# One decoder layer on one core: the attention and conv output projections in 512-column products, halves summed on the way out

## The chip, the core and the metric

The kernel runs on one core of a Trainium2 chip. The core has a matrix engine (PE, with its weight loads shown as PEld), a vector engine (DVE), a scalar engine (ACT), GpSimd (POOL) and a queue engine (SP) that issues the loads. PE reads operands from SBUF and writes results to PSUM, of which the kernel uses eight banks, each 512 float32 values wide on 128 partitions. DVE and ACT read PSUM and work through their instructions strictly in the order of the program; so does PE. The engines wait for each other by semaphores.

The metric is the device time of one execution in microseconds (us), as the median of several runs.

## What is computed

One layer of a hybrid decoder on 256 tokens of width 1024, in float32:

```python
proj  = x @ w_in[l]                   # q, k, v, B, C, h and two gates
y_att = moba_attention(q, k, v) @ w_attn_out[l]
y_cnv = (gate_b * causal_dwconv(gate_c * h_in, conv_w_mix[l])) @ w_conv_out[l]
mix   = (g_att * y_att + g_cnv * y_cnv) @ w_o[l]
x     = layer_norm(DEEPNORM_ALPHA * x + mix, ln1_g[l], ln1_b[l])
u     = causal_dwconv(x @ w_up[l], conv_w_ffn[l])
f     = (jax.nn.silu(u[..., :D_FF]) * u[..., D_FF:]) @ w_down[l]
x     = layer_norm(DEEPNORM_ALPHA * x + f, ln2_g[l], ln2_b[l])
```

The attention has 8 heads of 64, and with 256 tokens a single causal block. The change concerns `y_att`, `y_cnv` and the gated sum of the two.

## The kernel before

**Products in three parts.** Every float32 operand is split into a high part (ACT copies it into the type `fp32r`) and a low part (DVE subtracts the high part from the original). A product is then high x high + high x low + low x high, added up in PSUM. For an operand b of 256 tokens there are two forms. The plain one issues three products of 256 columns for each block of 128 rows of the contraction. The other (`cols_wide`, line 333, and `cols_narrow`, line 340) needs b's high and low parts side by side: one product of 512 columns multiplies the weight's high part with both, so that the bank's columns 0 to 255 take high x high and 256 to 511 take high x low; a second product of 256 columns adds low x high to the first half. Whoever empties the bank must add the two halves: ACT copies the second half out, DVE adds the first to it. The input projections for conv and gates and the feed-forward's up projection use this form before the change; the output projections of attention and conv use the plain one.

**Weights.** All weights come in a fixed order of units of 128 x 1024 values, two to a load of 1 MB into one of three raw buffers (line 175, on SP's queue). Splitting a unit takes an ACT copy (`split_h`, line 192, or line 219 by way of `hl_split`) and a DVE subtraction (`split_l`, line 197, or line 220). Nine buffers each hold the high and the low parts. A raw buffer is loaded anew when both units in it are split. In the order of units stand: the gates' 16 units; four pairs `ao`, `co`, `ao`, `co` (attention's and conv's output weights, each unit 512 rows by 256 columns), eight units of W_o, the first four up units, the rest of the feed-forward.

**The order by hand.** The program is written in slots, one for each unit; a slot issues its PE products, then weight copies on ACT and weight low parts on DVE for units some four or five ahead, then what is registered for it by `at` (ACT's part ahead of the weight copies, DVE's behind the low parts). In the gates' slots this is the sum of a gate's halves (lines 648 and 652) and the sigmoid (line 655).

**The stage of the change.** Lines 701 to 714: eight banks y0 to y7, each 128 output columns of both branches for all 256 tokens. `unit_cols` fills columns 256 to 511 of a bank with conv's part (12 products of 256 columns) and then columns 0 to 255 with attention's (12 more). Ahead of a bank the loop issues the splits due (`ahead`) and, for the bank two before, the split of its result (`mix_hl`). Behind it `mix` multiplies the bank by both gates on DVE straight from PSUM (line 694) and adds the two halves (line 695). The result is split into `mT`. The inputs are `aT` (attention, lines 460 to 468) and `yT` (conv, lines 624 to 628), each laid out as part, block, token.

Then come the W_o products for tokens 0 to 127 (eight units, two banks, six products a unit), in whose loop the splits for the coming units and the last two `mix_hl` are issued; the residual and the first layer norm of these rows on DVE (lines 742 to 726) beside the W_o products of tokens 128 to 255; the transposes of the normalized x1 (line 786) and the first up products.

**PSUM.** Four banks (`acc`) hold accumulations that stay long, four (`ps`) serve everything short: scores, transposes, the y banks. Ahead of the feed-forward the four are given back and opened anew as two pairs of banks (`ps_pair`).

Of the kernel before, what the change touches and what calls it, by code (L numbers as in the profile page):

```python
# [137 lines left out]
def layer_kernel(ctx: ExitStack, tc: tile.TileContext, x, wpack, cpack, ln1_g, ln1_b, ln2_g, ln2_b, out):  # L138
    nc = tc.nc

    cst = ctx.enter_context(tc.tile_pool(name="cst", bufs=1))
    big = ctx.enter_context(tc.tile_pool(name="big", bufs=1))
# [3 lines left out]
    single = ExitStack()  # L146
# [61 lines left out]
    def split(u, eng=None):  # L208
        if u < len(units) and units[u]["h"] is None:
            split_start(u)  # L210
            split_part(u, 0, units[u]["shape"][0], eng)
        elif u < len(units) and units[u]["l"] is None:
            split_l(u)

    def low(l, src, h):
        nc.vector.tensor_tensor(l, src, h.bitcast(F32), op=ALU.subtract)

    def hl_split(h, l, src, eng=None):
        nc.scalar.activation(h, src, AF.Copy)  # L219
        (eng or nc.vector).tensor_tensor(l, src, h.bitcast(F32), op=ALU.subtract)  # L220
# [94 lines left out]
                mm3(banks[t], ah[:, k0 + k, t * P:(t + 1) * P], al[:, k0 + k, t * P:(t + 1) * P],  # L315
                    un["h"][:, k, :], un["l"][:, k, :], first and k == 0, last and k == nk - 1)

    def unit_cols(u, o, bh, bl, n0=0):

        un = units[u]  # L320
        nk = un["shape"][0]
        for k in range(nk):
            wh, wl = un["h"][:, k, n0:n0 + P], un["l"][:, k, n0:n0 + P]
            nc.tensor.matmul(o, wh, bh[:, k, :], start=k == 0, stop=False)  # L324
            nc.tensor.matmul(o, wh, bl[:, k, :], start=False, stop=False)  # L325
            nc.tensor.matmul(o, wl, bh[:, k, :], start=False, stop=k == nk - 1)  # L326

    def cols_wide(u, bank, b):


        un = units[u]
        for k in range(un["h"].shape[1]):
            nc.tensor.matmul(bank, un["h"][:, k, :], b[:, k].rearrange("p a s -> p (a s)"), start=k == 0, stop=False)  # L333

    def cols_narrow(u, bank, b):

        un = units[u]
        nk = un["l"].shape[1]
        for k in range(nk):
            nc.tensor.matmul(bank[:, 0:S], un["l"][:, k, :], b[:, k, 0], start=False, stop=k == nk - 1)  # L340

    def cols_pair(u, second, banks, b):

# [3 lines left out]
            cols_narrow(u, banks[1], b)  # L347

    LA = 4
    cur = {"u": 0}  # L350

    def ahead(u):
        for v in range(cur["u"], u + LA + 1):
            split(v)
        cur["u"] = max(cur["u"], u + LA + 1)


    qk = big.tile([P, 2, 2, AW], F32, tag="rows", name="qk")
# [1 line left out]
    vpt = big.tile([P, 3584], F32R, tag="c16", name="vpt")  # L360
    vp = vpt[:, 0:2048].rearrange("p (a t n) -> p a t n", a=2, t=2)
    PT = vpt[:, 2048:3584].rearrange("p (a j n) -> p a j n", a=2, j=2)
    aT = big.tile([P, 2, 4, S], F32R, tag="d8", name="aT")
    yT = big.tile([P, 2, 4, S], F32R, tag="e8", name="yT")

    def rope(t):
        xv = qk[:, t].rearrange("p a (h d) -> p (a h) d", d=HD)[:, :, 0:16].rearrange("p h (i f) -> p h i f", i=2)
# [27 lines left out]
    SB, SM, PR = {}, {}, {}  # L395
# [64 lines left out]
    def attend_h(p):  # L460
        for j in range(2):
            hs = slice(j * HD, (j + 1) * HD)
            nc.scalar.activation(aT[hs, 0, p, :], PR[p, "o"][hs, j * 256:(j + 1) * 256], AF.Copy)

    def attend_l(p):
        for j in range(2):
            hs = slice(j * HD, (j + 1) * HD)
            low(aT[hs, 1, p, :], PR[p, "o"][hs, j * 256:(j + 1) * 256], aT[hs, 0, p, :])

# [4 lines left out]
    def at(u, part, f, *a):  # L474
        beside.setdefault(u, {}).setdefault(part, []).append((f, a))

    done = {"h": 0, "l": 0}

    def slot(u, products=None):


        if products:
            products()
        mine = beside.pop(u, {})
        for f, a in mine.get("pe", []) + mine.get("act", []):
            f(*a)
        while done["h"] <= u + LA + 1:
            if units[done["h"]]["h"] is None:
                split_h(done["h"])
            done["h"] += 1  # L490
        while done["l"] <= u + LA:
            if units[done["l"]]["l"] is None:
                split_l(done["l"])
            done["l"] += 1
        for f, a in mine.get("dve", []):
            f(*a)
# [18 lines left out]
    for p in range(4):  # L515
        s = C0 + 4 + 3 * p
# [3 lines left out]
        s = C0 + 7 + 5 * p  # L520
# [28 lines left out]
    banks = [[acc_bank(f"{m}{t}") for t in range(2)] for m in "qk"] + [[ps_bank(f"v{t}") for t in range(2)]]  # L549
# [40 lines left out]
    CB = {}  # L590
# [31 lines left out]
        nc.vector.tensor_tensor(t, CB["s", "b", pr], t, op=ALU.mult)  # L622

    def conv4_act(pr):
        nc.scalar.activation(yT[:, 0, 2 * pr:2 * pr + 2, :], CB["t", pr], AF.Copy)

    def conv4_dve(pr):
        low(yT[:, 1, 2 * pr:2 * pr + 2, :], CB["t", pr], yT[:, 0, 2 * pr:2 * pr + 2, :])

    for pr, (c1, c2, c3, c4) in enumerate(((6, 10, 11, 13), (13, 16, 18, 21))):  # L630
        at(C0 + c1, "dve", conv1, pr)
# [12 lines left out]
    gates = None  # L644
# [12 lines left out]
    for j in range(16):  # L657
        u = U[("g", 0)] + j
# [15 lines left out]
    for j in range(0, 16, 2):  # L674
        if j == 2:
            gates = big.tile([P, 8, 2, S], F32, tag="b16", name="gates")
        GB[j], GB[j + 1] = two_units(U[("g", 0)] + j, [f"g{j + e}" for e in range(2)])

    for e in range(2):
        slot(U[("g", 0)] + 16 + e)  # L680
    cur["u"] = done["l"]


    ln1 = big.tile([P, 2, D], F32, tag="d8", name="ln1")
    for i, g in enumerate((ln1_g, ln1_b)):
# [1 line left out]

    mT = big.tile([P, 2, KT, S], F32R, tag="c16", name="mT")

    M = {}  # L690

    def mix(i, bank):
        t = scratch([P, 2, S], f"m{i}")
        nc.vector.tensor_tensor(t, gates[:, i], bank.rearrange("p (a t) -> p a t", a=2), op=ALU.mult)
        nc.vector.tensor_tensor(t[:, 0], t[:, 0], t[:, 1], op=ALU.add)
        M[i] = t[:, 0]

    def mix_hl(i):
        hl_split(mT[:, 0, i, :], mT[:, 1, i, :], M.pop(i))

    for half in range(2):
        for e in range(2):
            ua, uc = U[("ao", half)] + e, U[("co", half)] + e
            for n in range(2):
                i = half * 4 + e * 2 + n
                if i > 1:
                    mix_hl(i - 2)
                ahead(uc + n - 1)
                bank = ps_bank(f"y{i}")
                unit_cols(uc, bank[:, 256:512], yT[:, 0], yT[:, 1], n * P)  # L710
                unit_cols(ua, bank[:, 0:256], aT[:, 0], aT[:, 1], n * P)
                if i == 0:
                    slot(uc + n)
                mix(i, bank)


    def norm_stats(r, stats, pieces):
# [43 lines left out]
    st1 = [tmp.tile([P, 4, 6], F32, tag="stats", name=f"stats{t}", bufs=2) for t in range(2)]  # L761
    banks = [acc_bank(f"o0{nh}") for nh in range(2)]
    for k in range(8):
        for v in range(cur["u"], min(U["wo"] + k + LA + 1, U["up0"] + 1)):
            split(v)
            cur["u"] = v + 1
        wo_rows(k, 0, banks)
        if k < 2:
            mix_hl(6 + k)
    for nh in range(2):  # L770
        residual(0, nh, banks[nh], xr, r1[0], st1[0], nh, nh * 512, nh * 512 + 512)
    norm1(0, r1[0], st1[0])
# [6 lines left out]
    for k in range(4, 8):  # L779
        wo_rows(k, 1, banks, (0,))  # L780

    def x1_transpose(t, cs=(0, 1)):
        for c in cs:
            b = ps_bank(f"x1t{t}{c}")
            for j in range(4):
                nc.tensor.transpose(b[:, j * P:(j + 1) * P], x1[:, t, (4 * c + j) * P:(4 * c + j + 1) * P], ident)
            hl_split(x1T[:, 4 * c:4 * c + 4, 0, t * P:(t + 1) * P], x1T[:, 4 * c:4 * c + 4, 1, t * P:(t + 1) * P],
                     b.rearrange("p (j t) -> p j t", j=4))
# [60 lines left out]
        wo_rows(k, 1, banks, (1,))  # L849
    residual(1, 1, banks[1], xr, r1[1], st1[1], 1, 512, 1024)  # L850
    norm1(1, r1[1], st1[1])
    cur["u"] = U["up0"] + 4
    u0 = U["up0"]
    rows = {}

    def up0_rows(t):
        bank = acc_bank("up0_1") if t else ps_bank("up0_0")
        for c in range(4):
            if t == 0 and c == 3:
                x1_transpose(1, (0,))  # L860
            unit_rows(u0 + c, 2 * c, {t: bank}, x1T[:, :, 0], x1T[:, :, 1], c == 0, c == 3, ts=(t,))
        rr = scratch([P, 512], f"up0r_{t}")
        rows[t] = rr
        return bank, rr
# [3 lines left out]
    nc.scalar.activation(r0, b0, AF.Copy)  # L868
    for v in range(4, 8):
        split(u0 + v)  # L870
    cur["u"] = u0 + 8
    b1, r1 = up0_rows(1)
    nc.scalar.activation(r1, b1, AF.Copy)
    for i in range(2):
        PB[i] = acc_bank(f"pb{i}")
    single.close()
    pairs = ctx.enter_context(tc.tile_pool(name="pairs", bufs=2, space=bass.MemoryType.PSUM))

    def ps_pair(name):
        return pairs.tile([P, 2, 512], F32, tag="pair", name=name)  # L880

    def up0_T(i):
        for a in range(2):
# [33 lines left out]
    seq = []  # L917
    for c in range(1, NP // 2):
        for e in range(2):
            i = 2 * c + e  # L920
# [4 lines left out]
                seq.append(("d", d, U[("dn", d // 2)] + d % 2))  # L925
    for d in range(NP - TAIL, NP):
        seq.append(("t", d, U[("dn", d // 2)] + d % 2))
    done = {"h": cur["u"] - seq[0][2], "l": cur["u"] - seq[0][2]}
    def slot(k, stages):


# [114 lines left out]
```

## Time and profile before

| | us |
|---|---|
| median of 3 runs (lowest, highest) | 368.86 (368.48, 370.68) |
| the profiled execution | 369.0 |
| its span in the trace | 367.1 |
| PE busy | 358.0 |
| DVE busy | 294.9 |
| ACT busy | 217.0 |

The time of an execution is a little longer than the span that the trace covers. The profile's lines name the kernel's line (L333), the engine, the operation, and output and inputs by the program's names without their numbers, so that `y` stands for all of y0 to y7. In a timeline the first number is the start in us from the span's start and the second the length of the entry, which may hold several instructions (x2, x3); square brackets give idle time of the engine ahead of it and what ended that.

### The profile page before, as it was taken

Reading aid. Unit: us, or ns where it says so; the run is one execution under the profiler, and the core shown is the slowest. Engines: PE = TensorE matmul, PEld = TensorE weight load, DVE = VectorE, ACT = ScalarE, POOL = GpSimd, SP = SyncE. Lnnn points to the kernel's source line nnn. Section 1 sums busy time; section 2 is a strip of 40 time slices with the busy share of each in tenths; the row PEclk is TensorE's granted clock in tenths of the full one; section 3 lists DMA queues with packets and bytes.
Section 4 is the critical chain, followed back from the end, with each engine's and each line's share of the span. In section 5 each row is a group of like instructions: output and inputs, shape, how many; then the busy total and the mean of one; then the engine's idle time right before and its main releaser. Section 6 shows DMA issues by size and latency. Waiting matters only on the chain.

```text
span 367.1 us, 5335 instructions
## 1 busy us (share of the span) xinstructions
PE 358.0 (98%) x2022; PEld 312.2 (85%) x2022; DVE 294.9 (80%) x510; ACT 217.0 (59%) x372; POOL 7.0 (2%) x26
## 2 busy tenths in 40 slices
PE   8999999999999999999999999999999999999991
PEld 7888888888888899988888888888888888888891
DVE  4696887788895679869769988987869696999784
ACT  4685776747867654634266666575657566676300
POOL 2000000000000000102000000000000000000000
PEclk9999999999999999999999999999999999999998
DMA  7978565333853634596360835448182645662011
GB/s 263 356 292 318 180 225 211 114 114 129 331 214 130 221 124 137 190 357 224 124 223 12 341 121 221 153 193 309 46 334 90 254 140 204 228 237 108 0 59 57
DMA packets 11241, 69.63 MB, mean 190 GB/s; under 512 B 1232, under 2 KB 1616, under 8 KB 4176
## 3 DMA queue, kind: packets, MB, share of 16 engines
q1 hardware_dynamic: 10496, 67.00, 50.0%
q0 software_dynamic: 576, 2.10, 1.8%
q8 instruction: 16, 0.26, 0.3%
q10 hardware_dynamic: 144, 0.20, 0.1%
q14 instruction: 9, 0.07, 0.1%
HBM read 68.24 MB, written 1.05 MB: 189 GB/s over the span
## 4 chain that ended last, share of the span: by engine, by line
PE 97%; DVE 1%; DMA 1%; DVEq 0%; SPq 0%; issue 0%
PE pb L333 20%; PE pb L340 10%; PE g L333 8%; PE d L305 5%; PE d L306 5%; PE d L307 5%; PE g L340 4%; PE q L555 3%; PE k L555 3%; PE v L555 3%; PE b L333 2%; PE y L326 2%; PE y L325 2%; PE y L324 2%; PE c L333 2%; PE o L307 2%
## 5 line engine op out<-in xcount | busy, mean ns | idle before, releaser
L197 DVE TENSOR_TENSOR wl<-raw,wh 128x1024 fp32r<-128x1024 f32 x90 | 109.8, 1221 | 23.3 <-ACT wh L192 22.7
L192 ACT ACTIVATE wh<-raw 128x1024 fp32r<-128x1024 f32 x90 | 94.5, 1055 | 22.7 <-DMA raw<-in_wpack 22.6
L333 PE MATMUL pb<-x1T,wh 128*128 128x512 f32 x320 | 76.2, 390 | 0.0
L333 PEld LDWEIGHTS pb<-x1T,wh 128*128 128x128 f32 x320 | 59.7, 188 | 12.1
L220 DVE TENSOR_TENSOR wl<-raw,wh 128x1024 fp32r<-128x1024 f32 (+1 forms) x38 | 38.0, 1037 | 7.4 <-ACT wh L219 7.1
L340 PEld LDWEIGHTS pb<-x1T,wl 128*128 128x128 f32 x320 | 41.0, 191 | 1.6
L340 PE MATMUL pb<-x1T,wl 128*128 128x256 f32 x320 | 41.5, 283 | 0.0
L219 ACT ACTIVATE wh<-raw 128x1024 fp32r<-128x1024 f32 (+1 forms) x38 | 32.9, 904 | 14.3 <-DMA raw<-in_wpack 8.5
L333 PE MATMUL g<-xT,wh 128*128 128x512 f32 x128 | 31.4, 393 | 0.0
L305 PE MATMUL d<-wh,f 128*128 128x512 f32 x80 | 31.3, 391 | 0.0
L306 PE MATMUL d<-wl,f 128*128 128x512 f32 x80 | 31.3, 391 | 0.0
L307 PE MATMUL d<-wh,f 128*128 128x512 f32 x80 | 31.1, 389 | 0.0
L333 PEld LDWEIGHTS g<-xT,wh 128*128 128x128 f32 x128 | 23.3, 188 | 4.5
L807 ACT ACTIVATE fb<-pb 128x512 f32<-128x512 f32 x20 | 11.9, 595 | 23.8 <-PE pb L340 23.8
L825 DVE SCALAR_TENSOR_TENSOR fc<-fb,consts,fc 128x254 f32<-128x254 f32 x40 | 19.3, 484 | 1.4
L823 DVE SCALAR_TENSOR_TENSOR fc<-fb,consts,fc 128x255 f32<-128x255 f32 x40 | 19.1, 478 | 0.0
L817 ACT ACTIVATE fc<-fb,consts 128x256 f32<-128x256 f32 x40 | 17.9, 496 | 0.4 <-DVE fb L811 0.4
L307 PEld LDWEIGHTS d<-wh,f 128*128 128x128 f32 x80 | 15.0, 188 | 3.2
L305 PEld LDWEIGHTS d<-wh,f 128*128 128x128 f32 x80 | 15.1, 189 | 2.7
L306 PEld LDWEIGHTS d<-wl,f 128*128 128x128 f32 x80 | 15.1, 189 | 2.6
L340 PEld LDWEIGHTS g<-xT,wl 128*128 128x128 f32 x128 | 16.4, 191 | 0.6
L340 PE MATMUL g<-xT,wl 128*128 128x256 f32 x128 | 16.6, 283 | 0.0
(183 smaller groups left out, 606.1 us busy)
## 6 DMA issues: line engine op xcount, KB each, us to landing
raw<-in_wpack SPq DMA_DIRECT2D x55, 1024.0 KB, 4.9
raw<-in_wpack SPq DMA_DIRECT2D x6, 896.0 KB, 5.5
xr<-in_x SPq DMA_DIRECT2D x1, 1024.0 KB, 7.6
ln<-in_ln_g POOLq DMA_DIRECT2D x2, 512.0 KB, 5.6
ln<-in_ln_b POOLq DMA_DIRECT2D x2, 512.0 KB, 6.2
raw<-in_wpack SPq DMA_DIRECT2D x3, 256.0 KB, 3.4
raw<-in_wpack SPq DMA_DIRECT2D x1, 512.0 KB, 5.8
out<-x SPq DMA_DIRECT2D x2, 256.0 KB, 2.1
```

What stands on the lines that cost most here:

```text
L192: nc.scalar.activation(units[u]["h"], raw_of(u), AF.Copy)
L197: nc.vector.tensor_tensor(units[u]["l"], raw_of(u), units[u]["h"].bitcast(F32), op=ALU.subtract)
L219: nc.scalar.activation(h, src, AF.Copy)
L220: (eng or nc.vector).tensor_tensor(l, src, h.bitcast(F32), op=ALU.subtract)
L305: nc.tensor.matmul(o, ah, bh, start=start, stop=False)
L306: nc.tensor.matmul(o, ah, bl, start=False, stop=False)
L307: nc.tensor.matmul(o, al, bh, start=False, stop=stop)
L333: nc.tensor.matmul(bank, un["h"][:, k, :], b[:, k].rearrange("p a s -> p (a s)"), start=k == 0, stop=False)
L340: nc.tensor.matmul(bank[:, 0:S], un["l"][:, k, :], b[:, k, 0], start=False, stop=k == nk - 1)
L555: nc.tensor.matmul(banks[m][t], (xl if p == 2 else xh)[:, k, t * P:(t + 1) * P], wl if p == 1 else wh, start=k == 0 and p == 0, stop=k == ...
L823: nc.vector.scalar_tensor_tensor(c[:, 1:S], pb[:, a * S:a * S + S - 1], w_ffn(1, j), c[:, 1:S], op0=ALU.mult, op1=ALU.add)
L825: nc.vector.scalar_tensor_tensor(c[:, 2:S], pb[:, a * S:a * S + S - 2], w_ffn(0, j), c[:, 2:S], op0=ALU.mult, op1=ALU.add)
```

## The change

The y banks go over to the wide and narrow form. Each y now takes a pair of banks, conv's in the second and attention's in the first, in 8 products of 512 columns and 8 of 256. ACT copies the second halves of both banks into a scratch tile (`mix_act`), DVE adds the first halves (`mix_sum`), multiplies by the gates and adds the branches (`mix_dve`); ACT and DVE split the result (`mix_h`, `mix_l`). `aT` and `yT` are laid out as block, part, token, so that the two parts lie side by side.

The stage is written as slots like those ahead of it: bank i's copy, sum and gating belong to the slot of bank i+1, its split to that of bank i+2. A new list `first` puts the sum ahead of the weight low parts of its slot. The two slots without products that stood ahead of the first bank go. The W_o loop for tokens 0 to 127 becomes slots too; splitting stops at the first up unit as before (`SPLIT_LAST`). The four short banks are given back and opened as two pairs ahead of the y stage instead of ahead of the feed-forward, and the transposes of x1 and the first up bank use halves of such pairs.

```diff
-    def cols_wide(u, bank, b):
+    def cols_wide(u, bank, b, n0=0):
...
-            nc.tensor.matmul(bank, un["h"][:, k, :], b[:, k].rearrange("p a s -> p (a s)"), start=k == 0, stop=False)
+            nc.tensor.matmul(bank, un["h"][:, k, n0:n0 + P], b[:, k].rearrange("p a s -> p (a s)"), start=k == 0, stop=False)
...
-            nc.tensor.matmul(bank[:, 0:S], un["l"][:, k, :], b[:, k, 0], start=False, stop=k == nk - 1)
+            nc.tensor.matmul(bank[:, 0:S], un["l"][:, k, n0:n0 + P], b[:, k, 0], start=False, stop=k == nk - 1)
...
-    aT = big.tile([P, 2, 4, S], F32R, tag="d8", name="aT")
-    yT = big.tile([P, 2, 4, S], F32R, tag="e8", name="yT")
+    aT = big.tile([P, 4, 2, S], F32R, tag="d8", name="aT")
+    yT = big.tile([P, 4, 2, S], F32R, tag="e8", name="yT")
...
+    SPLIT_LAST = U["up0"]
...
-        while done["h"] <= u + LA + 1:
+        while done["h"] <= min(u + LA + 1, SPLIT_LAST):
...
-        while done["l"] <= u + LA:
+        for f, a in mine.get("first", []):
+            f(*a)
+        while done["l"] <= min(u + LA, SPLIT_LAST):
...
-    for e in range(2):
-        slot(U[("g", 0)] + 16 + e)
-    cur["u"] = done["l"]
...
+    single.close()
+    pairs = ctx.enter_context(tc.tile_pool(name="pairs", bufs=2, space=bass.MemoryType.PSUM))
...
-    def mix(i, bank):
-        t = scratch([P, 2, S], f"m{i}")
-        nc.vector.tensor_tensor(t, gates[:, i], bank.rearrange("p (a t) -> p a t", a=2), op=ALU.mult)
+    def mix_act(i):
+
+        t = M["t", i] = scratch([P, 2, S], f"m{i}")
+        nc.scalar.activation(t, M[i][:, :, S:2 * S], AF.Copy)
+
+    def mix_sum(i):
+        t = M["t", i]
+        nc.vector.tensor_tensor(t, M.pop(i)[:, :, 0:S], t, op=ALU.add)
+
+    def mix_dve(i):
+        t = M["t", i]
+        nc.vector.tensor_tensor(t, gates[:, i], t, op=ALU.mult)
         nc.vector.tensor_tensor(t[:, 0], t[:, 0], t[:, 1], op=ALU.add)
...
+    def mix_h(i):
+        nc.scalar.activation(mT[:, 0, i, :], M["t", i][:, 0], AF.Copy)
+
+    def mix_l(i):
+        low(mT[:, 1, i, :], M.pop(("t", i))[:, 0], mT[:, 0, i, :])
...
+    def mixed(i):
+
+        M[i] = ps_pair(f"y{i}")
+        half, e, n0 = i // 4, i // 2 % 2, i % 2 * P
+        parts = [(U[("co", half)] + e, M[i][:, 1], yT, n0), (U[("ao", half)] + e, M[i][:, 0], aT, n0)]
+        if i == 0:
+            for part in parts:
+                cols_wide(*part)
+                cols_narrow(*part)
+        else:
+            for f in (cols_wide, cols_narrow):
+                for part in parts:
+                    f(*part)
+
+    for i in range(8):
+        at(Y0 + i + 1, "act", mix_act, i)
+        at(Y0 + i + 1, "first", mix_sum, i)
+        at(Y0 + i + 1, "dve", mix_dve, i)
+    for i in range(8):
+        at(Y0 + i + 2, "act", mix_h, i)
+        at(Y0 + i + 2, "dve", mix_l, i)
+    for i in range(8):
+        slot(Y0 + i, lambda: mixed(i))
...
-        for v in range(cur["u"], min(U["wo"] + k + LA + 1, U["up0"] + 1)):
-            split(v)
-            cur["u"] = v + 1
-        wo_rows(k, 0, banks)
-        if k < 2:
-            mix_hl(6 + k)
+        slot(U["wo"] + k, lambda: wo_rows(k, 0, banks))
...
+        if t not in XT:
+            XT[t] = ps_pair(f"x1t{t}")
         for c in cs:
-            b = ps_bank(f"x1t{t}{c}")
+            b = XT[t][:, c]
```

More of the change, by code (lines that the diff above doesn't have):

```diff
@@ L316, in unit_rows, with cols_narrow @@
                     un["h"][:, k, :], un["l"][:, k, :], first and k == 0, last and k == nk - 1)
[L318 to L326, printed above, removed]
-    def cols_wide(u, bank, b):
+    def cols_wide(u, bank, b, n0=0):
         un = units[u]
         for k in range(un["h"].shape[1]):
-            nc.tensor.matmul(bank, un["h"][:, k, :], b[:, k].rearrange("p a s -> p (a s)"), start=k == 0, stop=False)
-    def cols_narrow(u, bank, b):
+            nc.tensor.matmul(bank, un["h"][:, k, n0:n0 + P], b[:, k].rearrange("p a s -> p (a s)"), start=k == 0, stop=False)
+    def cols_narrow(u, bank, b, n0=0):
         un = units[u]
@@ L349, in layer_kernel @@
     LA = 4
-    cur = {"u": 0}
-    def ahead(u):
-        for v in range(cur["u"], u + LA + 1):
-            split(v)
-        cur["u"] = max(cur["u"], u + LA + 1)
     qk = big.tile([P, 2, 2, AW], F32, tag="rows", name="qk")
@@ L462, in attend_h @@
             hs = slice(j * HD, (j + 1) * HD)
-            nc.scalar.activation(aT[hs, 0, p, :], PR[p, "o"][hs, j * 256:(j + 1) * 256], AF.Copy)
+            nc.scalar.activation(aT[hs, p, 0, :], PR[p, "o"][hs, j * 256:(j + 1) * 256], AF.Copy)
     def attend_l(p):
@@ L467, in attend_l @@
             hs = slice(j * HD, (j + 1) * HD)
-            low(aT[hs, 1, p, :], PR[p, "o"][hs, j * 256:(j + 1) * 256], aT[hs, 0, p, :])
+            low(aT[hs, p, 1, :], PR[p, "o"][hs, j * 256:(j + 1) * 256], aT[hs, p, 0, :])
     beside = {}
@@ L624, in conv4_act @@
     def conv4_act(pr):
-        nc.scalar.activation(yT[:, 0, 2 * pr:2 * pr + 2, :], CB["t", pr], AF.Copy)
+        nc.scalar.activation(yT[:, 2 * pr:2 * pr + 2, 0, :], CB["t", pr], AF.Copy)
     def conv4_dve(pr):
-        low(yT[:, 1, 2 * pr:2 * pr + 2, :], CB["t", pr], yT[:, 0, 2 * pr:2 * pr + 2, :])
+        low(yT[:, 2 * pr:2 * pr + 2, 1, :], CB["t", pr], yT[:, 2 * pr:2 * pr + 2, 0, :])
     for pr, (c1, c2, c3, c4) in enumerate(((6, 10, 11, 13), (13, 16, 18, 21))):
@@ L688, in layer_kernel, with ps_pair @@
     mT = big.tile([P, 2, KT, S], F32R, tag="c16", name="mT")
+    single.close()
+    pairs = ctx.enter_context(tc.tile_pool(name="pairs", bufs=2, space=bass.MemoryType.PSUM))
+    def ps_pair(name):
+        return pairs.tile([P, 2, 512], F32, tag="pair", name=name)
     M = {}
-    def mix(i, bank):
-        t = scratch([P, 2, S], f"m{i}")
-        nc.vector.tensor_tensor(t, gates[:, i], bank.rearrange("p (a t) -> p a t", a=2), op=ALU.mult)
-        nc.vector.tensor_tensor(t[:, 0], t[:, 0], t[:, 1], op=ALU.add)
-        M[i] = t[:, 0]
@@ L698, in mix_hl @@
[L698 to L714, printed above, removed]
+    def mix_act(i):
+        t = M["t", i] = scratch([P, 2, S], f"m{i}")
+        nc.scalar.activation(t, M[i][:, :, S:2 * S], AF.Copy)
@@ new lines, in mix_sum @@
+    def mix_sum(i):
[4 more added lines that the diff above has]
+        nc.vector.tensor_tensor(t, gates[:, i], t, op=ALU.mult)
+        nc.vector.tensor_tensor(t[:, 0], t[:, 0], t[:, 1], op=ALU.add)
+    def mix_h(i):
+        nc.scalar.activation(mT[:, 0, i, :], M["t", i][:, 0], AF.Copy)
+    def mix_l(i):
+        low(mT[:, 1, i, :], M.pop(("t", i))[:, 0], mT[:, 0, i, :])
+    Y0 = U[("ao", 0)]
+    def mixed(i):
[10 more added lines that the diff above has]
+                    f(*part)
@@ L763, in layer_kernel @@
     for k in range(8):
-        for v in range(cur["u"], min(U["wo"] + k + LA + 1, U["up0"] + 1)):
-            split(v)
-            cur["u"] = v + 1
-        wo_rows(k, 0, banks)
-        if k < 2:
-            mix_hl(6 + k)
+        slot(U["wo"] + k, lambda: wo_rows(k, 0, banks))
     for nh in range(2):
@@ L780, in layer_kernel @@
         wo_rows(k, 1, banks, (0,))
+    XT = {}
     def x1_transpose(t, cs=(0, 1)):
+        if t not in XT:
+            XT[t] = ps_pair(f"x1t{t}")
         for c in cs:
-            b = ps_bank(f"x1t{t}{c}")
+            b = XT[t][:, c]
             for j in range(4):
@@ L851, in layer_kernel @@
     norm1(1, r1[1], st1[1])
-    cur["u"] = U["up0"] + 4
     u0 = U["up0"]
@@ L856, in up0_rows @@
     def up0_rows(t):
-        bank = acc_bank("up0_1") if t else ps_bank("up0_0")
+        bank = acc_bank("up0_1") if t else ps_pair("up0_0")[:, 0]
         for c in range(4):
@@ L870, in layer_kernel @@
         split(u0 + v)
-    cur["u"] = u0 + 8
     b1, r1 = up0_rows(1)
@@ L875, in layer_kernel @@
         PB[i] = acc_bank(f"pb{i}")
[L876 to L880, printed above, removed]
     def up0_T(i):
@@ L927, in layer_kernel @@
         seq.append(("t", d, U[("dn", d // 2)] + d % 2))
-    done = {"h": cur["u"] - seq[0][2], "l": cur["u"] - seq[0][2]}
+    done = {"h": u0 + 8 - seq[0][2], "l": u0 + 8 - seq[0][2]}
     def slot(k, stages):
```

## The prediction

> **What bounds the kernel now.** I read the page's busy line and its chain of waits first, then the list of who waited for whom on PE, then the stages around the change by windows.
>
> ```profile
> PE 358.0 (98%) x2022; PEld 312.2 (85%) x2022; DVE 294.9 (80%) x510; ACT 217.0 (59%) x372; POOL 7.0 (2%) x26
> ...
> PE 97%; DVE 1%; DMA 1%; DVEq 0%; SPq 0%; issue 0%
> ```
> ```profile
> PE warm L234 <- DVE zeros L224: 1.0, 1, 1.0
> PE q L555 <- DVE wh L564: 0.4, 1, 0.4
> ```
> ```profile
> 129.16:152.20 23.04, 23.04 (x195) 23.04 (x194) 18.75 (x30) 12.55 (x19) 0.00 (x0) 1.00 0.40 138
> 152.20:163.10 10.90, 10.90 (x51) 9.04 (x50) 7.87 (x11) 4.87 (x6) 1.25 (x2) 1.00 0.88 328
> ```
>
> 97% of the chain is PE, and after the start PE waits for nobody. So a microsecond taken from PE's instruction stream is a microsecond of the span, as long as the other engines keep up. The two windows are the stage that is changed (the eight y products, 129.16 to 152.20) and the W_o products of the first 128 rows behind it (to 163.10). Their columns after the range are length, PE, PEld, DVE, ACT, POOL, clock, DMA share and GB/s. The clock is full. DVE is busy 18.75 of 23.04 us and 7.87 of 10.90: it has 7.3 us to spare in the two together, and that is the quantity to watch.
>
> **PE's part.** Before, a y bank takes 24 products of 256 columns; after, 8 of 512 and 8 of 256.
>
> ```profile
> 129.16 0.19 PEld L324 LDWEIGHTS y<-yT,wh 128*128 128x128 f32 x1
> ...
> 152.20 0.19 PEld L305 LDWEIGHTS o<-wh,mT 128*128 128x128 f32 x1
> ```
> ```profile
> 193.44 3.65 PE pb L333 x16
> 197.10 1.91 PE pb L340 x16
> 199.01 0.23 PE d L305
> ```
>
> 192 products go by in 23.04 us: 0.120 each, 2.88 a bank. The same two helpers in the feed-forward stage show the new forms: 16 wide ones in 3.66 us (0.2288 each), 16 narrow ones in 1.91 (0.1194). A new bank is 8 x 0.2288 + 8 x 0.1194 = 2.78 us; eight are 22.24. PE's stream gets 0.80 us shorter and no more: the same 768 columns per row block pass the array, and only the cost of more, shorter instructions goes. The Trainium skill, "TensorE: Matmul & The Clock Gate", section "Wait — 56ns, not 53.3ns?", gives a warm product N / 2.4 GHz + about 2.5 ns, so that merging 64 pairs would save an estimated 0.16 us and the forecast below would end 0.1 higher. The rows differ from that: two narrow ones take 0.240 here against 0.229, and I go by them.
>
> **What DVE and ACT get.** Each bank now needs an ACT copy of its low halves (128x512 out of PSUM) and a DVE sum of the same size ahead of the gate multiplication. These exist in the feed-forward stage, as L807 and L811.
>
> ```profile
> L807 ACT ACTIVATE fb<-pb 128x512 f32<-128x512 f32 x20 | 11.9, 595 | 23.8 <-PE pb L340 23.8
> ```
> ```profile
> 144.66 0.68 DVE L694 TENSOR_TENSOR m<-gates,y 128x512 f32<-128x512 f32 x1
> 145.38 0.42 DVE L695 TENSOR_TENSOR m<-m 128x256 f32<-128x256 f32 x1
> 145.72 0.42 DVE L220 TENSOR_TENSOR mT<-m,mT 128x256 fp32r<-128x256 f32 x1
> 146.06 1.22 DVE L220 TENSOR_TENSOR wl<-raw,wh 128x1024 fp32r<-128x1024 f32 x1
> 147.19 0.68 DVE L694 TENSOR_TENSOR m<-gates,y 128x512 f32<-128x512 f32 x1
> ```
> ```profile
> 200.55 0.68 DVE L811 TENSOR_TENSOR fb<-pb,fb 128x512 f32<-128x512 f32 x1
> 201.15 0.42 DVE L834 TENSOR_TENSOR ff<-fs,fc 128x256 f32<-128x256 f32 x1
> ```
>
> I count DVE by the distance from start to start, since an instruction starts before the one ahead has its recorded end. By the rows: sum 0.60 (200.55 to 201.15), gate multiplication 0.72 (its follower needs its result), addition 0.34, low part of mT 0.34, weight low part 1.13. One bank with its weight split cost DVE 2.53 us; it will cost 3.13. That is more than PE's 2.78: in steady state DVE, not PE, sets the pace. ACT gets 0.60 more a bank, beside a weight copy and the copy of mT:
>
> ```profile
> 134.09 0.42 ACT L219 ACTIVATE mT<-m 128x256 fp32r<-128x256 f32 x1 [1.00 <-DVE m L695]
> ...
> 151.14 1.05 ACT L219 ACTIVATE wh<-raw 128x1024 fp32r<-128x1024 f32 x1
> ```
>
> 0.60 + 0.42 + 1.05 = 2.07 us against 2.78, so it holds nobody by its load.
>
> The pool matters too. Before, four single banks took y in turn; after, two pairs do, so product i+2 can't start before the sum of bank i has read its pair. That sum is first in its DVE slot, and the slots come at 3.13 us.
>
> **Start of the stage.** Times are those of the profile before. DVE's state at 129.16, and the delay from a bank's last product to its reader:
>
> ```profile
> 129.56 0.42 DVE L652 TENSOR_TENSOR gs<-g,gs 128x256 f32<-128x256 f32 x1
> 130.03 1.23 DVE L197 TENSOR_TENSOR wl<-raw,wh 128x1024 fp32r<-128x1024 f32 x1
> 131.18 0.42 DVE L652 TENSOR_TENSOR gs<-g,gs 128x256 f32<-128x256 f32 x1
> ```
> ```profile
> 134.91 0.28 PE L326 MATMUL y<-aT,wl 128*128 128x256 f32 x1
> 134.92 0.19 PEld L324 LDWEIGHTS y<-yT,wh 128*128 128x128 f32 x1
> ...
> 135.24 0.69 DVE L694 TENSOR_TENSOR m<-gates,y 128x512 f32<-128x512 f32 x1 [1.18 <-PE y L326]
> ```
>
> A reader starts 0.32 us after PE has gone on to the next bank. Product 0 ends at 129.16 + 2.78 = 131.94, its ACT copy runs 132.26 to 132.86, its DVE sum starts at 132.90. Before, DVE used that time for the weight split at 130.03 and the gate sum at 131.18; after, both stand in the queue behind the sum (the slot's order: sum, weight split, the rest). So DVE idles from 129.98 to 132.90, and the 7.3 us of room shrink by 2.9.
>
> **The sum.** What stands in DVE's queue from 132.90 to the first residual of the W_o result, which must follow it all: 8 sums x 0.60 = 4.80; 12 weight splits (from the sixth unit of this block to the first up unit) x 1.13 = 13.56; one gate sum 0.34; 8 multiplications x 0.72 = 5.76; 8 additions and 8 low parts x 0.34 = 5.44. Together 29.90, and about 0.1 where the second sum waits for ACT, which is held by the last gate. DVE is free at 162.90.
>
> ```profile
> 156.52 3.49 DVE L220 TENSOR_TENSOR wl<-raw,wh 128x1024 fp32r<-128x1024 f32 x3
> 162.74 0.69 DVE L742 SCALAR_TENSOR_TENSOR xr<-xr,o 128x512 f32<-128x512 f32 x1 [2.73 <-PE o L307]
> ```
>
> Before, that residual began at 162.74 after 2.73 us of idling. So DVE arrives 0.16 us late instead of 2.7 early.
>
> PE by the same pace: products 0 to 4 run back to back, product 5 waits for sum 3, and 6 and 7 for sums 4 and 5. Sum k starts at 132.90 + 3.13 per slot (plus the 0.1) and takes 0.69: sum 5 ends at 149.34, product 7 starts at 149.39 and ends at 152.17. The stage ends where it ended before (152.20); the 0.80 us is returned as three waits. The W_o products then run at 10.90 us, with about 0.1 of waiting each at the sixth and the seventh for the weight low parts that DVE makes 1.13 apart: they end at 163.27 against 163.10.
>
> From there on the work is the old work, 0.17 us later.
>
> ```profile
> 177.97 0.75 DVE L726 SCALAR_TENSOR_TENSOR x<-x,mv,ln 128x512 f32<-128x512 f32 x1
> 178.64 0.75 DVE L725 SCALAR_TENSOR_TENSOR x<-xr,mv,ln 128x512 f32<-128x512 f32 x1
> ```
> ```profile
> 179.10 0.27 PE L786 MATMUL x1t<-ident,x 128*128 128x128 f32 x1
> ```
>
> The second normalization ends its first half at 178.72 and PE reads it at 179.10: 0.38 us would hide a lag of DVE alone, but here PE shifts with it. The result is the profiled execution's 369.0 (span 367.1 and 1.9 around it) + 0.2 = **369.2 us**. The profiled time lies 0.1 above the median 368.86.
>
> **Edits I cost at nothing.** The other order of aT and yT changes strides, not sizes. The pair pool opened early needs its four banks free; their last reader is the low part of the last attention output:
>
> ```profile
> 126.52 0.86 DVE L216 TENSOR_TENSOR aT<-av,aT 64x256 fp32r<-64x256 f32 x2 [1.99 <-ACT aT L463]
> ```
>
> It is done at 127.38, ahead of 129.16 (if that cover went, product 0 would wait by as much). The transposes of x1 in a pair's halves touch separate banks, read as before. The first W_o row pass takes its splits after its products instead of ahead, which on ACT and DVE is the same queue; ACT runs one unit further ahead. The splits issue the weight loads, so these move too:
>
> ```profile
> 151.03 1.22 DVE L220 TENSOR_TENSOR wl<-raw,wh 128x1024 fp32r<-128x1024 f32 x1
> ...
> 152.28 36.33 SPq L175 DMA_DIRECT2D raw<-in_wpack  x7
> ```
> ```profile
> 157.13 1.06 ACT L219 ACTIVATE wh<-raw 128x1024 fp32r<-128x1024 f32 x1 [1.12 <-DMA raw<-in_wpack]
> ```
>
> The load of the first up units starts when the low part of the fourth W_o unit is done (152.25 before, by my slots 153.6 after), and lands 4.85 us later, 158.5; ACT wants it near 160.2 and DVE at 161.8. That cover is 1.7 us; beyond it each microsecond delays the residual by one, less the 0.38.
>
> **The rivals.**
> - *PE keeps its gain.* The multiplication now reads SBUF only, and sits between others than before. The nearest row of such a multiplication with an independent follower:
>
> ```profile
> 76.56 0.68 DVE L622 TENSOR_TENSOR ct<-cb,ct 128x512 f32<-128x512 f32 x1
> 77.17 0.41 DVE L600 TENSOR_TENSOR cc<-c,cc 128x256 f32<-128x256 f32 x1
> ```
>
>  0.61. At 0.60 a slot is 3.01 and the queue 0.96 shorter: the W_o products end 0.5 earlier, 368.5. The floor is PE's whole 0.80: 368.2. Against it: the addition right behind still needs the product's result, as at 144.66. Chance 0.22.
> - *DVE is the bound, clearly slower.* If each instruction costs its recorded duration (0.69, 1.22, 0.72, 0.42, 0.42) the slot is 3.47 and the queue behind 132.90 becomes 33.1 us instead of 29.9: 372.2. It decides from a queue of 29.8, where DVE stops arriving in time. If only the sum takes 0.72, as L694 does, it is +1.1: 370.1. The Trainium skill, "VectorE: DVE Perf Modes", section "The DRAIN you can't avoid", says that the next operation doesn't start until the pipe has emptied, which leans this way. The traces don't bear out the full price: the follower of L811 starts 0.60 after it where its duration is 0.68. Chance 0.25.
> - *ACT holds the copy.* It is strictly in order behind the weight copies; a late load such as the 1.12 us wait at 157.13, if it falls on a y slot, would pass to DVE's queue whole: 370.3. In this stage no ACT copy waits for a load before, and the loads land several us ahead. Chance 0.06.
>
> **Numbers.** The forecast (368.8 to 369.8) has the remaining 0.47. The range reaches from the floor of the first rival to most of the second: 368.2 to 371.2; about 0.13 is above it, 0.04 below. From no change a measurement of this kernel tells about 1% (3.7 us). The gain can't exceed 0.8 us unless something outside these stages moves: faster 0.01. Slower by over 1% needs more than the second rival's full price: 0.06. Within 1%: 0.93.
>
> **What would show it.** PE waiting on the new sum at about three of the y products, 0.3 us each, all late in the stage; sums 3.1 us apart; no idle time of DVE ahead of the first residual where it had 2.73; y stage still about 23 us. Sums at 2.78 apart with no PE wait mean the first rival; at 3.4 apart, the second. I am wrong in kind if PE waits before the third product, at the opening of the pair pool, or in the feed-forward stage.

## The result and the profile after

| | us |
|---|---|
| before, median of 6 runs | 368.83 (368.43 to 370.68) |
| after, median of 6 runs | 374.52 (373.17 to 375.40) |
| ratio, 95% interval | 1.0148 (1.0129 to 1.0167) |
| profiled execution after, and its span | 374.43, 372.7 |

The change makes the kernel 5.7 us slower, outside the range of the prediction. The busy line and the chain of the page after show PE as busy as before, but no longer alone on the chain:

```profile
PE 359.7 (97%) x1958; PEld 309.1 (83%) x1958; DVE 299.2 (80%) x518; ACT 221.6 (59%) x380; POOL 7.0 (2%) x26
...
PE 85%; DVE 10%; DMA 3%; ACT 0%; issue 0%; POOL 0%; DVEq 0%; SPq 0%; POOLq 0%
```

Who waited for whom on PE (total, times, longest) has a new line at the top:

```profile
PE x1t L797 <- DVE x1T L220: 3.7, 1, 3.7
PE warm L234 <- DVE zeros L224: 1.0, 1, 1.0
PE q L543 <- DVE wh L552: 0.4, 1, 0.4
```

It isn't in the y stage. `x1t` are the transposes of the first layer norm's result, 19 us behind the y products. PE's timeline there, after the change:

```profile
171.26 0.60 PE L797 MATMUL x1t<-ident,x 128*128 128x128 f32 x4
175.57 1.11 PE L797 MATMUL x1t<-ident,x 128*128 128x128 f32 x4 [3.71 <-DVE x1T L220]
176.33 0.78 PE L305 MATMUL o<-wh,mT 128*128 128x512 f32 x1
176.91 0.63 PE L306 MATMUL o<-wl,mT 128*128 128x512 f32 x1
177.33 0.63 PE L307 MATMUL o<-wh,mT 128*128 128x512 f32 x1
177.76 0.63 PE L305 MATMUL o<-wh,mT 128*128 128x512 f32 x1
```

Before, all eight transposes went in one row:

```profile
171.38 1.03 PE L786 MATMUL x1t<-ident,x 128*128 128x128 f32 x8
172.18 0.47 PE L305 MATMUL o<-wh,mT 128*128 128x512 f32 x1
172.49 0.39 PE L306 MATMUL o<-wl,mT 128*128 128x512 f32 x1
172.72 0.40 PE L307 MATMUL o<-wh,mT 128*128 128x512 f32 x1
```

After, PE issues the first four, then idles 3.7 us, then issues the other four, and the W_o products behind them start 0.43 us apart instead of 0.23. The windows (columns as in the prediction) give the granted clock, that is the share of PE's full clock that the trace reports: 0.52, and full again from 178.8:

```profile
175.50:178.80 3.30, 3.23 (x10) 2.75 (x11) 0.70 (x2) 0.60 (x1) 0.00 (x0) 0.52 0.70 295
178.80:185.00 6.20, 6.20 (x31) 5.13 (x30) 4.27 (x7) 0.00 (x1) 0.57 (x1) 1.00 0.01 3
```

What released PE is a DVE subtraction, and DVE's timeline says why that was so late. It is the low part of the first half's transposes, and it stands behind three weight low parts and the residual of the other row block:

```profile
169.91 3.49 DVE L220 TENSOR_TENSOR wl<-raw,wh 128x1024 fp32r<-128x1024 f32 x3
173.32 0.68 DVE L754 SCALAR_TENSOR_TENSOR xr<-xr,o 128x512 f32<-128x512 f32 x1
174.03 0.69 DVE L756 BATCH_NORM_STATS2 stats<-xr 128x6 f32<-128x512 f32 x1
174.76 0.15 DVE L751 TENSOR_SCALAR stats<-stats 128x1 f32<-128x1 f32 x1
174.83 0.68 DVE L220 TENSOR_TENSOR x1T<-x1t,x1T 128x512 fp32r<-128x512 f32 x1
```

Before, that subtraction ran at 174.20, both halves in one entry:

```profile
174.20 1.28 DVE L220 TENSOR_TENSOR x1T<-x1t,x1T 128x512 fp32r<-128x512 f32 x2
```

Counted from the first y product of each trace (129.16 before, 128.83 after) it came 45.04 us behind it before and 46.00 after, so DVE was only 1.0 us earlier before. But then the second half had a bank of its own, and nobody waited. After, both halves are banks of one pair, and the trace names the first half's subtraction as what the second half's first transpose waited for (`3.71 <-DVE x1T L220`).

The y stage itself came out as worked out. DVE's slot there, from sum to sum:

```profile
138.94 0.68 DVE L689 TENSOR_TENSOR m<-y,m 128x512 f32<-128x512 f32 x1
139.54 1.21 DVE L197 TENSOR_TENSOR wl<-raw,wh 128x1024 fp32r<-128x1024 f32 x1
140.68 0.68 DVE L693 TENSOR_TENSOR m<-gates,m 128x512 f32<-128x512 f32 x1
141.39 0.43 DVE L694 TENSOR_TENSOR m<-m 128x256 f32<-128x256 f32 x1
141.74 0.42 DVE L216 TENSOR_TENSOR mT<-m,mT 128x256 fp32r<-128x256 f32 x1
142.07 0.68 DVE L689 TENSOR_TENSOR m<-y,m 128x512 f32<-128x512 f32 x1
```

138.94 to 142.07 is 3.13 us.

This table of stages is read from PE's weight loads in each trace (the first one of each stage). It leaves out what lies ahead of the first y product, which begins between 128.2 and 131.1 us in the ten traces here. Behind the last column the rest of the kernel takes 180.5 to 180.6 us in every trace.

| us | y stage | W_o to x1 transposes | transposes to up products | up products to the rest | sum |
|---|---|---|---|---|---|
| before | 23.04 | 18.96 | 3.64 | 11.81 | 57.45 |
| after | 23.04 | 19.16 | 9.02 | 12.08 | 63.30 |

Of the 5.85 us, 5.38 lie at the first row block's transposes: 3.87 us more from the first four to the second four (4.31 against 0.44), and 1.5 us more from there to the up products. Another 0.27 lies in the last stage, where the second row block's transposes come, and 0.20 in the W_o stage.

### The profile page after: what moved, and what is told of

It is laid out like the page before. It is cut to its first block, busy times and chain, and to the rows that moved or that the text cites. A ratio compares the mean times of both kernels' runs of the same rounds, so it can differ in the third digit from the quotient of the medians.

```text
span 372.7 us, 5212 instructions
## 1 busy us (share of the span) xinstructions
PE 359.7 (97%) x1958; PEld 309.1 (83%) x1958; DVE 299.2 (80%) x518; ACT 221.6 (59%) x380; POOL 7.0 (2%) x26
## 4 chain that ended last, share of the span: by engine, by line
PE 85%; DVE 10%; DMA 3%; ACT 0%; issue 0%; POOL 0%; DVEq 0%; SPq 0%; POOLq 0%
PE pb L323 20%; PE pb L330 10%; PE g L323 8%; PE d L305 5%; PE d L306 5%; PE d L307 5%; PE g L330 4%; PE q L543 3%; PE k L543 3%; PE v L543 3%; DMA raw<-in_wpack 3%; DVE wl L197 2%; PE b L323 2%; PE c L323 2%; PE h L323 2%; DVE m L689 1%
## 5 line engine op out<-in xcount | busy, mean ns | idle before, releaser
L197 DVE TENSOR_TENSOR wl<-raw,wh 128x1024 fp32r<-128x1024 f32 x99 | 120.7, 1221 | 24.1 <-ACT wh L192 23.5
L192 ACT ACTIVATE wh<-raw 128x1024 fp32r<-128x1024 f32 x99 | 103.8, 1054 | 25.0 <-DMA raw<-in_wpack 25.0
L220 DVE TENSOR_TENSOR wl<-raw,wh 128x1024 fp32r<-128x1024 f32 (+1 forms) x29 | 27.3, 982 | 7.4 <-ACT wh L219 7.2
L219 ACT ACTIVATE wh<-raw 128x1024 fp32r<-128x1024 f32 (+1 forms) x29 | 23.6, 858 | 8.3 <-DMA raw<-in_wpack 7.3
```

Source lines behind the costliest of these rows:

```text
L192: nc.scalar.activation(units[u]["h"], raw_of(u), AF.Copy)
L197: nc.vector.tensor_tensor(units[u]["l"], raw_of(u), units[u]["h"].bitcast(F32), op=ALU.subtract)
```

## The experiments

The theory "shared pair" says that PE waits because the two halves of a row block's transposes are parts of one pair, and that the slow clock behind it follows from the idling. The rival "DVE late" says that DVE, fuller since the y stage, would hold PE up there in any case.

**e1_own_pairs** takes the shared pair away and leaves all else of the change.

```diff
-        if t not in XT:
-            XT[t] = ps_pair(f"x1t{t}")
         for c in cs:
-            b = XT[t][:, c]
+            b = ps_pair(f"x1t{t}{c}")[:, 0]
...
-        bank = acc_bank("up0_1") if t else ps_pair("up0_0")[:, 0]
+        bank = acc_bank(f"up0_{t}")
```

> The changed kernel, but each half of the x1 transposes takes a pair of its own (one bank of it used) and the first up bank goes to the long-lived banks. Theory 'shared pair': the 3.7 us wait of PE ahead of the second four transposes, the 1.7 us of slow products behind it and the 0.2 us at the second row block come from a wait for DVE's reading of the other half of the same pair; they all go, and the time is 369.2 (368.8 to 369.6), 0.2 above the kernel before. Rival 'DVE late': DVE's fuller queue out of the y stage reaches PE at the transposes in any case; then most of the 5.6 us stays, 373 or more.

Measured: 369.71 us (12 runs), ratio to before 1.0022 (1.0006 to 1.0037). The eight transposes go in one row again:

```profile
171.20 1.03 PE L795 MATMUL x1t<-ident,x 128*128 128x128 f32 x8
```

The stages are 23.03, 19.17, 3.64 and 12.18, sum 58.02. "DVE late" falls as a cause on its own: DVE has the same work, its first subtraction comes 45.81 us behind the first y product (45.04 before), and the wait is gone. The time is 0.1 above the expected range. By the stages 0.57 us above before remains, 0.4 more than the 0.17 forecast for the y stage.

**e2_pairs_only** is the kernel before with the pool opened as pairs ahead of the transposes and the halves put in one pair (the first up bank takes half of a pair too, as in the change).

```diff
+    single.close()
+    pairs = ctx.enter_context(tc.tile_pool(name="pairs", bufs=2, space=bass.MemoryType.PSUM))
...
         for c in cs:
-            b = ps_bank(f"x1t{t}{c}")
+            b = XT[t][:, c]
```

> The kernel before with one part of the change alone: the four short banks are opened as two pairs ahead of the x1 transposes, and the two halves of a row block share a pair; the y stage stays as it was. 'Shared pair': the wait comes here too, about 3.7 us and slow products behind it, 374.3 (373 to 375.5). 'DVE late': nothing of the y stage has changed, so 368.9 (within 0.4).

Measured: 375.69 us (4 runs, 372.46 to 375.90), ratio 1.0153 (1.0107 to 1.0199). The wait is there, 2.95 us of idling, and the clock behind it is 0.62 over 3.2 us:

```profile
173.31 0.60 PE L796 MATMUL x1t<-ident,x 128*128 128x128 f32 x4
176.86 0.66 PE L796 MATMUL x1t<-ident,x 128*128 128x128 f32 x4 [2.95 <-DVE x1T L220]
```
```profile
176.80:180.00 3.20, 3.14 (x11) 2.60 (x12) 0.70 (x2) 0.60 (x1) 0.00 (x0) 0.62 0.73 297
```

The sum of the stages is 62.46, 5.0 above before, of which 4.75 at the first transposes. So this one edit, without any of the change in the y stage, brings most of the loss. DVE's subtraction comes 45.04 us behind the first y product here, exactly as before, and the wait is 2.95 us instead of the 3.71 after the change: the 1.0 us by which DVE is later after the change lengthens the wait by 0.8. That much of "DVE late" is true, but only through the shared pair. The median lies 0.2 above the expected range. The profiled execution's 375.9 holds 1.9 us more that lie ahead of the y stage, where nothing was edited, mostly in its first 11 us: its first products ran 0.43 us apart until 10.7, those of the kernel before until 6.5. The granted clock reads 1.00 there in both traces, so why they were slow stays open.

**e3_fill** keeps the wait and keeps PE active in it.

```diff
+            if t == 0 and c == 1:
+                fill = acc_bank("fill")
+                for i in range(56):
+                    nc.tensor.matmul(fill[:, 0:P], zeros, zeros, start=True, stop=True)
             b = XT[t][:, c]
```

> The changed kernel with 56 small products of zeros on PE between the first and the second four transposes of the first row block (their result is not used); they fit into the wait. If the slow products behind the wait come from the clock dropping after PE idled, they go: the wait stays, the clock is about 0.997, the time 372.7 (1.7 less than 374.4). If they are slow for another reason (reads of PSUM or SBUF by the other engines at that moment), it stays at 374.4.

Measured: 373.33 us (6 runs, 372.49 to 374.92), ratio 1.0119 (1.0091 to 1.0147). PE around the wait, and the window behind it:

```profile
171.08 3.29 PE L798 MATMUL fill<-zeros 128*128 128x128 bf16 x56
175.35 0.66 PE L801 MATMUL x1t<-ident,x 128*128 128x128 f32 x4 [0.98 <-DVE x1T L220]
```
```profile
175.50:178.00 2.50, 2.50 (x14) 2.11 (x14) 0.69 (x1) 0.60 (x1) 0.00 (x0) 1.00 0.85 351
```

The clock is 1.00 where it was 0.52. From the second four transposes to the up products it takes 3.25 us (the stage's 7.96 less the 4.71 between the fours) instead of 4.71: the slow clock cost 1.5 us. The median moved by 1.2, not by the 1.7 expected. In the traces, the distance between the fours is 0.4 longer here (4.71 against 4.31), since DVE waited 1.10 us for the load of the first up units instead of 0.69. The slow products follow from the idling.

**e4_short_wait** lets DVE free the shared pair earlier.

```diff
+    x1_transpose(0, (0,))
     residual(1, 0, banks[0], xr, r1[1], st1[1], 0, 0, 512)
-    x1_transpose(0)
+    x1_transpose(0, (1,))
```

> The changed kernel with the residual of the second row block's first half moved behind the first half's transposes, so that DVE frees the shared pair 1.5 us earlier. 'Shared pair': the wait is 2.2 us instead of 3.7; 372.9 if the clock drops all the same, 371.2 if an idle time of 2.2 us leaves the clock alone. 'DVE late': DVE does the same work, 374.4.

Measured: 372.54 us (4 runs, 371.80 to 374.89), ratio 1.0108 (1.0069 to 1.0146).

```profile
174.43 0.66 PE L797 MATMUL x1t<-ident,x 128*128 128x128 f32 x4 [2.31 <-DVE x1T L220]
```
```profile
174.40:178.00 3.60, 3.57 (x18) 3.02 (x19) 2.13 (x5) 0.60 (x1) 0.00 (x0) 1.00 1.01 412
```

The wait became 2.31 us, as expected, and in this execution (371.85) the clock stayed full. The mean clock of the four runs is 0.993, 0.992, 0.989 and 0.988, with 371.85, 371.80, 374.89 and 373.23 us: it may have dropped behind the wait in the slower two, but only one of the four has a trace, so that isn't shown. The 371.8 of the two fastest is 0.6 above the 371.2 expected for a full clock.

The next four ask what holds the y stage at 23.0 us once the pair is out of the way. All build on e1_own_pairs.

**e5_pool_add** moves DVE's addition of the two branches to GpSimd.

```diff
-        nc.vector.tensor_tensor(t[:, 0], t[:, 0], t[:, 1], op=ALU.add)
+        nc.gpsimd.tensor_tensor(t[:, 0], t[:, 0], t[:, 1], op=ALU.add)
```

The loads of the first norm's constants, issued by GpSimd, go behind the y loop, because they wait for the last y product and the additions would stand behind them.

> The kernel with the transposes in pairs of their own, and the addition of the two branches moved from DVE to GpSimd (whose loads of the first layer norm's constants are issued behind the y stage for it). Theory 'DVE sets the pace': a DVE slot is 0.60 + 1.13 + 0.60 + 0.34 = 2.67 us instead of 3.13, below PE's 2.78; PE no longer waits, the y stage is 22.3 us instead of 23.03 and the time about 368.9, 0.8 less than with the addition on DVE. Rival 'something else holds the y stage at 23.0' (the two pairs, or ACT's copy): it stays at 23.0 and the time at 369.7. If GpSimd takes over 2 us for an addition or slows DVE, slower than 369.7.

Measured: **367.97 us** (12 runs), ratio 0.9980 (0.9964 to 0.9996). DVE's slot and GpSimd's addition:

```profile
138.02 0.68 DVE L685 TENSOR_TENSOR m<-y,m 128x512 f32<-128x512 f32 x1
138.62 1.21 DVE L197 TENSOR_TENSOR wl<-raw,wh 128x1024 fp32r<-128x1024 f32 x1
139.75 0.68 DVE L689 TENSOR_TENSOR m<-gates,m 128x512 f32<-128x512 f32 x1
140.36 0.42 DVE L216 TENSOR_TENSOR mT<-m,mT 128x256 fp32r<-128x256 f32 x1
140.69 0.68 DVE L685 TENSOR_TENSOR m<-y,m 128x512 f32<-128x512 f32 x1
```
```profile
140.52 0.86 POOL L690 TENSOR_TENSOR m<-m 128x256 f32<-128x256 f32 x1 [1.82 <-DVE m L689]
```

The slot is 2.67 us, the y stage 22.36, the sum of the stages 56.80: 0.65 below the kernel before. This beats both kernels, by little. The two pairs and ACT's copy are still there, so neither held the stage at 23.0. The time is 0.9 below the expected one: of the 1.22 that the stages fall below e1_own_pairs, 0.67 lie in the y stage and 0.55 behind it, where DVE is in time again (1.25 us of idling ahead of the first residual) and ACT no longer waits for the first up units. Their load is issued at 150.83 here, ahead of the constants' loads at 152.25. Since the edit moves those loads too, the shares of the two in the 0.55 aren't told apart.

**e6_early_slots** puts the two slots without products back ahead of the first bank.

```diff
+    for e in range(2):
+        slot(U[("g", 0)] + 16 + e)
```

> The kernel with the transposes in pairs of their own, and the two slots without products back ahead of the y stage, so that one weight low part and one gate sum fill DVE's 2.9 us of idling ahead of the first sum. 'DVE sets the pace': the sums come 0.45 us earlier from the third on, PE waits only once, the y stage is 22.6 us, the time 369.2. Rival: y stage 23.0, 369.7.

Measured: 369.65 us (12 runs), ratio 1.0024 (1.0009 to 1.0038). The y stage is 22.60 as expected, but the time is that of e1_own_pairs. Of the gain of 0.43, the stages hand 0.20 back in the last one (12.38 against 12.18), because DVE, done early, waits for ACT and ACT for a load (0.72 us; 0.52 in e1_own_pairs). The other 0.2 doesn't show in the medians.

```profile
159.17 2.35 DVE L197 TENSOR_TENSOR wl<-raw,wh 128x1024 fp32r<-128x1024 f32 x2
162.23 1.23 DVE L197 TENSOR_TENSOR wl<-raw,wh 128x1024 fp32r<-128x1024 f32 x1 [0.72 <-ACT wh L192]
163.37 0.68 DVE L757 SCALAR_TENSOR_TENSOR xr<-xr,o 128x512 f32<-128x512 f32 x1
```

**e7_both** has both edits.

> Both of these edits together. 'DVE sets the pace': y stage 22.3 us, DVE some 2 us ahead at the first residual again, no wait for the weight low parts in the W_o products and none at the second row block's transposes: 368.2, that is 0.6 below the kernel before. Rival: no better than 369.7.

Measured: 368.43 us (11 runs), ratio 0.9988 (0.9975 to 1.0002). The stages are those of e5_pool_add (22.36, 18.96, 3.64, 11.81), so the early slots add nothing there. The median is 0.46 above that of e5_pool_add; the stages don't show this, and in the traces it lies ahead of the y stage (first y product at 129.26 against 128.37). The expected 2 us of DVE's lead at the first residual came out as 1.25.

**e8_no_sum** leaves ACT's copy and DVE's sum out; the multiplication reads the first halves straight from PSUM. The multiplication and the addition also move to the front of their slot, ahead of the weight low parts, where the sum stood, because the multiplication now frees the pair.

```diff
-        nc.scalar.activation(t, M[i][:, :, S:2 * S], AF.Copy)
...
-        nc.vector.tensor_tensor(t, M.pop(i)[:, :, 0:S], t, op=ALU.add)
...
-        nc.vector.tensor_tensor(t, gates[:, i], t, op=ALU.mult)
+        nc.vector.tensor_tensor(t, gates[:, i], M.pop(i)[:, :, 0:S], op=ALU.mult)
...
-        at(Y0 + i + 1, "dve", mix_dve, i)
+        at(Y0 + i + 1, "first", mix_dve, i)
```

> The kernel with the transposes in pairs of their own, without ACT's copy and DVE's sum of the halves in the y stage: the gates multiply the first halves straight out of PSUM, and the high x low products are left out of the result. 'DVE sets the pace': y stage 22.2 to 22.3 us, DVE idle for 2 us or more ahead of the first residual, 368.3. Rival (pairs or the order of the products): 23.0, 369.7.

Measured: 368.37 us (10 runs), ratio 0.9986 (0.9974 to 0.9997). The y stage is 22.36, and DVE idles 2.73 us ahead of the first residual, as it did before the change:

```profile
161.97 0.69 DVE L752 SCALAR_TENSOR_TENSOR xr<-xr,o 128x512 f32<-128x512 f32 x1 [2.73 <-PE o L307]
```

So the wide form's whole gain on PE is 0.68 us. With e5_pool_add, which keeps the copy and the sum and only shortens DVE's slot, this shows that the sum of the halves, by lengthening DVE's slot, is what took the gain back.

## Why the prediction was wrong

- **PE's part was right, a little large.** A bank of 2.78 us makes 22.24 for eight; the y stage without waits is 22.36 (e5, e7, e8): 0.68 us gained instead of 0.80.
- **DVE's slot was right.** 3.13 us forecast, 3.13 measured; 2.67 forecast for e5 and measured. Counting from start to start rather than by recorded durations (3.47) was the step that decided this, so the rival "DVE is the bound, clearly slower" fell in its full price: the weight low part at 139.54 follows the 0.68 us sum at 138.94 after 0.60. The rule that leaned that way, in the Trainium skill, "VectorE: DVE Perf Modes", section "The DRAIN you can't avoid", has an exception in the same section, which the prediction left out: "A next op that is not held starts earlier". The trace agrees with the exception (0.60).
- **The y stage and W_o were right.** The y stage ends where it ended before (23.04 and 23.04); PE reaches the transposes 0.20 us late (19.16 against 18.96), forecast 0.17. Of the three waits forecast in the stage the trace names two, 0.5 us together. The rival "PE keeps its gain" fell: the multiplication's follower still waited for its result (140.68 to 141.39, 0.71). So did "ACT holds the copy": no copy of a y bank waited for a load.
- **The load for the first up units was mis-sized.** I gave it 4.85 us from issue to use and a cover of 1.7. It took 7.8:

```profile
153.34 7.77 DMA raw<-in_wpack
161.14 1.07 ACT wh L192
162.23 1.23 DVE wl L197
```

DVE waited 0.69 for it and began the residual at 163.38 where the sum, moved to this trace's y start (0.33 earlier), says 162.57. The two loads of the norm's constants were issued at 152.76 and 153.47, around it; before, they came 0.8 us behind it. The other traces go with this: in e1_own_pairs and e6_early_slots the constants' loads were again issued 0.6 us ahead, and the load took 7.6 and 7.8; in e8_no_sum they came 1.1 behind, and it took 5.0. No run moved them alone, so that they are the cause isn't shown. In the changed kernel the lag lengthens the wait at the transposes; in e1_own_pairs it is the last stage's 0.37, since the cover of 0.38 at the second row block is used up.
- **The step that failed** stands among the edits costed at nothing: "The transposes of x1 in a pair's halves touch separate banks, read as before." The banks are separate, but the waits are not made by banks here: the second half waits until the first half is read. That step was worth 5.4 us at the first row block and 0.27 at the second, where e2_pairs_only, which has the shared pair without the change of the y stage, has 4.75 and 0.26; the other 0.6 at the first row block came with DVE's lag. No rival held it. The profile before even had most of its price on show: the subtraction that would have to be waited for ran at 174.20 and took 0.69, and the second half's transposes began at 171.8. That is 3.1 us of delay, and e2_pairs_only measured 3.1 (3.55 us between the fours against 0.44). With a pair for each half (e1_own_pairs, 369.71) the time lies inside the forecast of 368.8 to 369.8. The signs I named as wrong in kind listed the opening of the pool and the feed-forward, not this place.
- **The clock** was no part of the sum at all. In the trace after, an idle time of 3.7 us is followed by half the clock for about 3 us, 1.5 us more. It may not come every time: two of the six executions after took 373.2 at a mean clock of 0.996, the other four 374.4 to 375.4 at 0.989 to 0.992, and the fastest of e2_pairs_only 372.46 at 0.997. The three faster ones have no traces, and the kernel before has mean clocks from 0.992 to 0.997 without such a wait, so this stays open. The Trainium skill, "TensorE: Matmul & The Clock Gate", section "HAM oscillation — how this bites in real kernels", warns of PE idle gaps above about 3.4 us. The trace after agrees (3.7 us, clock 0.52 behind it), and e4's 2.31 us left the clock full in its trace; but e2 lost it after 2.95 us (idle times by the trace, which models the ends of products), so the figure isn't a bound to rely on.

## What to carry to other kernels

When a change puts two short-lived results into parts of one buffer, list for each part who writes it and who must have read the other part first: if the parts are ordered as one buffer, as they were here, the price is the reader's place in its queue, which the old trace shows. Merging narrow products into wide ones gave PE only 0.01 us each here, while the sum of halves cost the next engine 0.60 us a bank; such an edit pays only where that engine's slot stays below PE's, so work out both slots from start-to-start distances. And price an idle time of PE of about 3 us with the slow products that followed it here, 1.5 us.

## What was not expected of the hardware

- In the traces the clock dropped to 0.52 after an idle time of 3.7 us and to 0.62 after 2.95 us, and stayed full after 2.31 us and where small products of zeros filled most of the wait.
- GpSimd's addition took 0.74 to 0.86 us where DVE's took 0.42, and slowed DVE little: the slot was 2.67 as computed. But one weight low part, started beside an addition on GpSimd, took 1.75 us instead of 1.22 in e5_pool_add (and 1.76 in e7_both at the same place):

```profile
154.42 1.75 DVE L197 TENSOR_TENSOR wl<-raw,wh 128x1024 fp32r<-128x1024 f32 x1
```
```profile
154.32 0.78 POOL L690 TENSOR_TENSOR m<-m 128x256 f32<-128x256 f32 x1 [0.80 <-DVE m L689]
```

Whether the two share a path into SBUF there wasn't tried. The slow low part accounts for 0.5 of the 0.75 us of lead that DVE lacked in e7_both.
